# A hybrid attention and recurrence layer on one core: pools at multiples of 2048 bytes, and a queue plan with other durations

## The chip, the cores and the metric

The kernel runs on one core of a Trainium2 chip. The metric is the device time of one execution in microseconds (us). The engines are TensorE (PE; its weight loads are shown as PEld), VectorE (DVE), ScalarE (ACT), GpSimd (POOL) and SyncE (SP), which here only issues loads and stores.

## What is computed

One layer over 512 latent tokens and 256 context tokens, model width 2048, in float32. Cut to what matters:

```
hn = rmsnorm(h) * (1 + scale) + shift          # scale, shift, gate: silu(c) @ w_ada + b_ada
q, k, v, g, a_f, a_b, r, gr, m8, m9 = split(hn @ w_in)   # 14368 columns, latent and context
o = gla_bidir(q, k, v, log_sigmoid(a @ w_gla_a) / 16)    # 4 heads, dk 256, dv 512, both directions
y = rglru_bidir(conv4(r))                      # 2048 channels, 16 blocks, scans in both directions
y_gla = (rmsnorm(o) * silu(g)) @ w_o_gla
y_lru = (y * silu(gr)) @ w_o_rnn
out = rmsnorm(x + gate * ((sigmoid(m8) * y_gla + sigmoid(m9) * y_lru) @ w_out))
```

The context tokens pass through the same weights, and their last scan states start the latent scans.

## The kernel before

Every large product is made from float32r halves: a value is split into hi and lo, and `mm3` (L129) adds three matmuls, hi x hi, hi x lo, lo x hi. Weights come in pieces of 128 x 1024 (512 KB). `run` (L210) walks over a list of pieces: it loads some ahead (on SyncE's queue, into two raw buffers), splits each two pieces before its matmuls (`hilo`, L119: ScalarE writes whi, VectorE writes wlo, into a ring of three), and runs the piece's matmuls. There are 304 such splits. 24 matmuls of 512 columns make a piece of the output product.

Besides these pieces there is side work: generators in `self.side` (`rnn_block`, `gla_all`, `gate_row`), from which `run_side` (L163) takes the next step at every `yield` of a piece's matmuls. Whether it takes one is decided by a plan of times `self.T` and `self.rdy`, in which each helper (`act`, `tt`, `ts`, `stt`, `scan`, `mm`) adds its duration: it stops where VectorE or ScalarE is more than `lim` ahead of TensorE, or where a result that the next step waits for is not ready by `slack`. These numbers change only the order in which instructions are put in the queues. `flush_side` (L199) takes all that is left.

The stages, in order:
- `start` (L460), with a plan of its own (`at`, `pe`, `hot`, `todo`, `idle`): 8 tiles of x and 4 of the context are loaded and squared, `sums` (L569) adds over the partitions with fp32 matmuls against ones, `rstd` and `spread` make the reciprocal root mean square for every token; 64 pieces of the ada weights give scale and shift (`ada`, `mod`); `modulate` writes xhi, xlo, chi and clo; the key product (`key`) fills in between. Eight slots of 512 KB hold ada pieces: four of araw, four of tok.
- The recurrence's stage: `g_feat` for r and gr (xhi or chi moving, weights stationary) and `g_tok` for the values (weights moving, xhi, xlo, chi or clo stationary, 256 columns), with `rnn_block` as side work.
- The attention's stage: query, gates and the merge gates as pieces, `gla_all` as side work, head after head. `swap` (L408), called when the first piece of y is reloaded, flushes what is left of it.
- `g_out` for both branches, then `g_final` (L1487): four blocks j of 512 output columns, 8 pieces each. At j = 0 `loads` (L1501) fetches x in pieces 0 to 3 and three broadcast rows (gt, the gate; gb, its bias; gf, the last norm's gain) in pieces 4 to 6; GpSimd adds gb to gt in piece 6. `evac` (L1518) does for each of four token tiles: y = product * gt, x + y, the squares' sum on ScalarE, and for j < 3 the product with gf. Block 3 is finished tile by tile (`finish`, L1571).

SBUF pools lie one behind the other: const, raw, ring, xp (xhi, xlo; later o and the output stage's tiles), sm (small tiles, 1088 bytes a partition), cx (chi, clo), then start, or rnn, or st and gla, or st and yp. raw, ring and xp begin at multiples of 2048 bytes; chi, rnn, st and gla begin 1088 bytes past one, and yp at one again, by an unused tile `fill` of 960 bytes (L413).

Of the kernel before, what the change touches and what calls it, by code (L numbers as in the profile page):

```python
# [54 lines left out]
class Kern:  # L55
# [27 lines left out]
    def act(self, out, in_, func=AF.Copy, **kw):  # L83
        t = self.TABLE.get(func, self.table)
        sw = 1.3 if t != self.table else 0.0
        self.table = t
        self._op("act", self._n(in_) / 1200.0 + 0.2 + sw, out, in_)
        if "accum_out" in kw:
            self.rdy[kw["accum_out"].name] = self.T["act"] + 0.1
        return self.nc.scalar.activation(out=out, in_=in_, func=func, **kw)  # L90

    def tt(self, out, in0, in1, op):
        self._op("dve", self._n(out) / 960.0 + 0.08, out, in0, in1)
        return self.nc.vector.tensor_tensor(out=out, in0=in0, in1=in1, op=op)  # L94

    def ts(self, out, in0, s1, s2=None, op0=ALU.mult, op1=None):
        self._op("dve", self._n(out) / 960.0 + 0.08, out, in0, s1)
        if op1 is None:
            return self.nc.vector.tensor_scalar(out=out, in0=in0, scalar1=s1, scalar2=None, op0=op0)
        return self.nc.vector.tensor_scalar(out=out, in0=in0, scalar1=s1, scalar2=s2, op0=op0, op1=op1)  # L100

    def stt(self, out, in0, s, in1, op0, op1):
        self._op("dve", self._n(out) / 960.0 + 0.08, out, in0, in1)
        return self.nc.vector.scalar_tensor_tensor(out=out, in0=in0, scalar=s, in1=in1, op0=op0, op1=op1)  # L104

    def scan(self, out, a, u, init):
        self._op("dve", self._n(out) / 480.0 + 0.08, out, a, u)
# [15 lines left out]
    def mm(self, out, lhsT, rhs, start, stop, share=1):  # L123

        n = self._n(rhs)
        self._op("pe", (n / 2400.0 + 0.003 if n >= 256 else 0.213) / share, out, lhsT, rhs)
        self.nc.tensor.matmul(out, lhsT=lhsT, rhs=rhs, start=start, stop=stop, skip_group_check=True)  # L127
# [175 lines left out]
    def build(self):  # L303
# [31 lines left out]
        self.cp = const.tile([P, 32], F32, name="cp")  # L335
        self.sm = open_pool("sm", bufs=2)

# [16 lines left out]
        def to_rnn():  # L354
# [6 lines left out]
            nc.gpsimd.memset(self.mask.rearrange("p (b t) -> p b t", t=P)[:, :, 0:1], 0.0)  # L361
            self.rp = open_pool("rnn", bufs=1)
            self.side.append(self.decay_consts())
            self.gacc = self.rp.tile([P, 1024], F32, tag="gacc", name="gacc")

# [42 lines left out]
        def swap():  # L408
            self.flush_side()
            close_pool("gla")  # L410
            self.yp = yp = open_pool("yp", bufs=1)

            yp.tile([P, 240], F32, name="fill")  # L413
            R["y"] = [yp.tile([P, KT, 512], F32R, tag=t, name=t) for t in ("yhi", "ylo")]
# [45 lines left out]
    def start(self, sp, raw0, raw, prime):  # L460
# [74 lines left out]
        sb_free = [0.0]  # L535
        pr0 = self.ps.tile([P, 4, 2], F32, tag="sb", name="pr")

# [4 lines left out]
        def squares(i, t):  # L542
            if i < 8:
                q = self.ring.tile([P, 1024], F32R, tag="whi", name="sq").bitcast(F32)
                h = self.ring.tile([P, 1024], F32R, tag="wlo", name="sh").bitcast(F32)[:, 0:512]
                nc.scalar.activation(out=q, in_=tok[i], func=AF.Square)
                e = at("act", 1.06, t)
                nc.vector.tensor_tensor(out=h, in0=q[:, 0:512], in1=q[:, 512:1024], op=ALU.add)
                f = at("dve", 0.7, e)
                hot.append((lambda: f, lambda: sums(i, h, f)))  # L550
                return
# [17 lines left out]
        def sums(i, h, r):  # L569

            for j in range(4):
                nc.tensor.matmul(pr0[:, j, :], lhsT=h[:, j * P:(j + 1) * P], rhs=ones[:, 0:2],
                                 start=i == 0 and j == 0, stop=i == 7, skip_group_check=True)
            t = pe("pr", 0.9, r)
            if i == 7:
# [8 lines left out]
        def rstd(s, pr, t):  # L584
            n = width[s] // P
            q = sp.tile([P, 4], F32, tag="rq", name="rq")[:, 0:n]
            self.rstd(q, pr[:, :, 0], D, sp.tile([P, 2, 4], F32, tag="rt", name="rt")[:, :, 0:n])
            t = sb_free[0] = at("dve", 0.4, t + 0.1)
            at("act", 0.2, t)
# [5 lines left out]
            t = at("dve", 0.22 * n, t)  # L595
            hot.append((lambda: max(t, sb_free[0]), lambda: spread(s, g, t)))

        def spread(s, g, r):

            w = width[s]  # L600
            pr = self.ps.tile([P, w], F32, tag="sb", name="pr")
            nc.tensor.matmul(pr, lhsT=ones, rhs=g[:, 0:w], start=True, stop=True)
            t = pe("pr", w / 600 + 0.05, r, sb_free[0])
            nc.scalar.activation(out=rms[s], in_=pr, func=AF.Copy)
            sb_free[0] = tok_ok[s] = at("act", w / 1200 + 0.18, t + 0.1)

# [305 lines left out]
    def evac_v(self, j):  # L912
        def f(c, x0, x1):
            h, o = j // 2, (j % 2) * 256
            for i, t in enumerate((c, x0, x1)):
                s = self.rp.tile([P, 2, 256], F32, tag="stg", name="vt", bufs=2)
                self.act(s, t)
# [137 lines left out]
    def gate_row(self, acc, hf):  # L1055
        nc = self.nc
        for j in range(2):
            row = self.rp.tile([1, 512], F32, tag="grow", name="grow")
            yield self.dep(acc)
# [427 lines left out]
    def g_final(self, j):  # L1487
# [30 lines left out]
        def evac(t, then=None):  # L1518
# [5 lines left out]
            if then:  # L1524
                then()
            self.act(self.junk, xr, AF.Square, accum_out=self.fss[:, t, j:j + 1])
            if j < 3:
                self.tt(xr, xr, self.gf[:, c0:c0 + 512], ALU.mult)

        held = []  # L1530
        for pi in range(8):
            def mm(hi, lo, pi=pi):
# [8 lines left out]
                if j == 0:  # L1541
                    loads(pi)
                if j == 0 and pi == 6:
                    nc.gpsimd.tensor_tensor(out=self.gt, in0=self.gt, in1=self.gb, op=ALU.add)
                if j == 3 and pi >= 5:
                    held.append((pi, hi, lo))
                    if pi == 7:
                        rest = None
                        for t in range(4):
# [5 lines left out]
                for t in range(4):  # L1555
                    mm_k(t, pi, hi, lo)

            def post():
                if j < 3:
                    for t in range(4):  # L1560
                        evac(t)
                if j == 2:

                    f = self.fss
                    self.fsum = self.sm.tile([P, 4], F32, tag="fsum", name="fsum")
                    self.tt(self.fsum, f[:, :, 0], f[:, :, 1], ALU.add)
                    self.stt(self.fsum, self.fsum, EPS * D, f[:, :, 2], ALU.add, ALU.add)
            ps.append(Piece(a["w"][W_OUT + 8 * j + pi], mm, post if pi == 7 else None))
# [106 lines left out]
```

## Time and profile before

| | us |
|---|---|
| timed, median of 3 (lowest to highest) | 2302.43 (2301.64 to 2302.9) |
| the profiled execution | 2307.69 |
| its span, first to last instruction | 2306.0 |
| TensorE busy in the span | 2275.4 (99%) |
| VectorE, ScalarE, GpSimd busy | 1163.2, 1016.3, 105.5 |

Busy time of TensorE is counted from modelled ends of pipelined matmuls, so 99% does not say how dense they are; that is read from the times between starts. The chain that ended last and the waits tell which engine a stretch hangs on; a wait is put down to what came last.

### The profile page before, as it was taken

The page shows a single profiled execution, that of the slowest core. Times are in us where ns is not written, and L with a number is a line of the kernel's source. Part 1 is how long each engine was busy: PE and PEld are TensorE (multiplying, and loading weights), DVE is VectorE, ACT ScalarE, POOL GpSimd, SP SyncE. Part 2 cuts the span into 40 slices and gives each one's busy share as a digit, 9 for nine tenths or more (in the row PEclk, how much of TensorE's full clock was granted, in tenths as well). Part 3 has the DMA queues.
Part 4 walks back from the last instruction along what each step waited for, and adds up shares of the span by engine and source line. Part 5 has one row for each costly group of instructions (what it writes and reads, how often), then busy time and mean ns, then how long its engine had stood idle before and what let it go on. Part 6 is the DMA issues. An engine that isn't in the chain of part 4 may idle for free. (4 is left out here: it accounts for less than half of the span.)

```text
span 2306.0 us, 29334 instructions
## 1 busy us (share of the span) xinstructions
PE 2275.4 (99%) x12064; PEld 1928.6 (84%) x12064; DVE 1163.2 (50%) x1494; ACT 1016.3 (44%) x1334; POOL 105.5 (5%) x201
## 2 busy tenths in 40 slices
PE   8999999999999999999999999999999999999998
PEld 5588889989898988998888888888888888888786
DVE  3563245655566555646637637647623432443335
ACT  4343255454454455456556555555533312222223
POOL 0010000000000000000000000000000000000000
PEclk9999999999999999999999999999999999999999
DMA  9943222333333332233233233323335533334423
GB/s 392 375 165 127 92 79 90 129 120 110 105 106 128 124 112 81 100 113 115 90 106 124 83 106 127 119 74 110 132 114 197 192 123 115 127 113 150 173 101 119
DMA packets 85814, 303.02 MB, mean 131 GB/s; under 512 B 10416, under 2 KB 11568, under 8 KB 84784
## 3 DMA queue, kind: packets, MB, share of 16 engines
q1 hardware_dynamic: 72656, 255.78, 32.0%
q0 software_dynamic: 13024, 45.37, 5.5%
q8 instruction: 94, 1.54, 0.3%
q14 instruction: 40, 0.33, 0.0%
HBM read 270.69 MB, written 30.42 MB: 131 GB/s over the span
## 5 line engine op out<-in xcount | busy, mean ns | idle before, releaser
L94 DVE TENSOR_TENSOR wlo<-raw,whi 128x1024 fp32r<-128x1024 f32 x304 | 371.9, 1224 | 568.1 <-ACT whi L90 566.8
L90 ACT ACTIVATE whi<-raw 128x1024 fp32r<-128x1024 f32 x304 | 321.0, 1057 | 529.8 <-PE px L127 327.3
L127 PE MATMUL px<-xhi,whi 128*128 128x512 f32 x1408 | 551.5, 392 | 0.0
L127 PE MATMUL px<-xhi,wlo 128*128 128x512 f32 x1408 | 549.1, 390 | 0.0
L127 PE MATMUL px<-xlo,whi 128*128 128x512 f32 x1408 | 548.1, 389 | 0.0
L127 PEld LDWEIGHTS px<-xhi,wlo 128*128 128x128 f32 x1408 | 264.2, 188 | 57.5 <-DVE wlo L94 0.2
L127 PEld LDWEIGHTS px<-xhi,whi 128*128 128x128 f32 x1408 | 264.4, 188 | 53.9 <-issue 2.6
L127 PEld LDWEIGHTS px<-xlo,whi 128*128 128x128 f32 x1408 | 264.5, 188 | 51.6
L127 PE MATMUL px<-whi,xhi 128*128 128x256 f32 x512 | 144.8, 283 | 0.0
L127 PE MATMUL px<-wlo,xhi 128*128 128x256 f32 x512 | 144.8, 283 | 0.0
L127 PE MATMUL px<-whi,xlo 128*128 128x256 f32 x512 | 144.7, 283 | 0.0
L90 ACT ACT_TABLE_LOAD x100 | 128.3, 1283 | 1.7
L127 PE MATMUL px<-whi,mhi 128*128 128x512 f32 x256 | 100.7, 393 | 2.3 <-ACT whi L90 2.3
L127 PE MATMUL px<-wlo,mhi 128*128 128x512 f32 x256 | 101.0, 394 | 0.8 <-DVE wlo L94 0.8
L127 PE MATMUL px<-whi,mlo 128*128 128x512 f32 x256 | 100.7, 393 | 0.0
L127 PE MATMUL px<-yhi,whi 128*128 128x512 f32 x256 | 99.6, 389 | 0.0
L127 PE MATMUL px<-ylo,whi 128*128 128x512 f32 x256 | 99.6, 389 | 0.0
L127 PE MATMUL px<-yhi,wlo 128*128 128x512 f32 x256 | 99.6, 389 | 0.0
L127 PE MATMUL px<-ohi,whi 128*128 128x512 f32 x256 | 99.6, 389 | 0.0
L127 PE MATMUL px<-olo,whi 128*128 128x512 f32 x256 | 99.6, 389 | 0.0
L127 PE MATMUL px<-ohi,wlo 128*128 128x512 f32 x256 | 99.6, 389 | 0.0
L127 PEld LDWEIGHTS px<-wlo,xhi 128*128 128x128 f32 x512 | 98.1, 192 | 0.2
(327 smaller groups left out, 3963.6 us busy)
## 6 DMA issues: line engine op xcount, KB each, us to landing
raw<-in_w SPq DMA_DIRECT2D x304, 512.0 KB, 3.6
araw<-in_wss SPq DMA_DIRECT2D x35, 512.0 KB, 8.9
raw<-in_wgt SPq DMA_DIRECT2D x32, 512.0 KB, 4.2
tok<-in_wss SPq DMA_DIRECT2D x29, 512.0 KB, 8.9
kraw<-in_w POOLq DMA_DIRECT2D x16, 512.0 KB, 3.9
gS<-mst POOLq DMA_DIRECT2D x32, 256.0 KB, 2.5
gst<-gS POOLq DMA_DIRECT2D x32, 256.0 KB, 3.0
vS<-vt POOLq DMA_DIRECT2D x24, 256.0 KB, 2.6
```

The source lines that it names most:

```text
L90: return self.nc.scalar.activation(out=out, in_=in_, func=func, **kw)
L94: return self.nc.vector.tensor_tensor(out=out, in0=in0, in1=in1, op=op)
L127: self.nc.tensor.matmul(out, lhsT=lhsT, rhs=rhs, start=start, stop=stop, skip_group_check=True)
```

## The change

It does five things.
- **Pools.** sm is opened on the right side of SBUF, so that cx and all that follows begin at multiples of 2048 bytes; `fill` goes; the rnn pool's tags are laid out in a fixed order, those of 512, 1024 and 768 columns each together.
- **Durations of the plan.** VectorE's fixed part rises from 0.08 to 0.16 (0.21 with a scalar operand), ScalarE's by 0.07 for each operand scale or bias, a matmul's from 0.003 to 0.0135.
- **Start.** Two tiles of x are added before the matmuls against ones: four groups of eight records instead of eight groups. Their result and the spread's for x use PSUM banks px instead of sb. The start's own durations are set anew (1.87 instead of 0.9 for a group).
- **Output stage's loads.** gt and gb are loaded in pieces 0 and 1, gf in piece 4, and GpSimd's add comes in piece 3.
- **Output stage's evacuation.** Blocks 0 to 2 make only y and x + y at their end; the squares and the product with gf become side work `squares()`, taken at `yield`s between the next block's matmuls.

```diff
@@ act, tt, ts, stt, scan, mm @@
-        self._op("act", self._n(in_) / 1200.0 + 0.2 + sw, out, in_)
+        ap = sum(not isinstance(kw.get(k, 0.0), (int, float)) for k in ("scale", "bias"))
+        self._op("act", self._n(in_) / 1200.0 + 0.2 + 0.07 * ap + sw, out, in_)
...
-        self._op("dve", self._n(out) / 960.0 + 0.08, out, in0, in1)
+        self._op("dve", self._n(out) / 960.0 + 0.16, out, in0, in1)
...
-        self._op("pe", (n / 2400.0 + 0.003 if n >= 256 else 0.213) / share, out, lhsT, rhs)
+        self._op("pe", (n / 2400.0 + 0.0135 if n >= 256 else 0.213) / share, out, lhsT, rhs)
@@ build @@
-        self.sm = open_pool("sm", bufs=2)
+        self.sm = open_pool("sm", bufs=2, side="right")
...
+            self.gacc = rp.tile([P, 1024], F32, tag="gacc", name="gacc")
+            for n, w, d, m in (("wh", 512, F32R, 1), ("wl", 512, F32R, 1), ("wr", 512, F32, 1), ("gr", TX, F32, 3),
+                               ("sgr", TX, F32, 2), ("stg", 512, F32, 2), ("grow", 512, F32, 1), ("xr", TA, F32, 3),
+                               ("xh", TA, F32R, 1), ("xc", TA, F32, 1), ("xl", TA, F32R, 1)):
+                rp.tile([P, w], d, tag=n, name=n + "0", bufs=m)
...
-            yp.tile([P, 240], F32, name="fill")
@@ start @@
-        pr0 = self.ps.tile([P, 4, 2], F32, tag="sb", name="pr")
+        pr0 = self.px.tile([P, 4, 2], F32, tag="px", name="pr")
...
-                h = self.ring.tile([P, 1024], F32R, tag="wlo", name="sh").bitcast(F32)[:, 0:512]
                 nc.scalar.activation(out=q, in_=tok[i], func=AF.Square)
                 e = at("act", 1.06, t)
-                nc.vector.tensor_tensor(out=h, in0=q[:, 0:512], in1=q[:, 512:1024], op=ALU.add)
-                f = at("dve", 0.7, e)
-                hot.append((lambda: f, lambda: sums(i, h, f)))
+                if i % 2 == 0:
+                    half.append(self.ring.tile([P, 1024], F32R, tag="wlo", name="sh").bitcast(F32)[:, 0:512])
+                    nc.vector.tensor_tensor(out=half[0], in0=q[:, 0:512], in1=q[:, 512:1024], op=ALU.add)
+                    at("dve", 0.7, e)
+                else:
+                    h = half.pop()
+                    for u in (q[:, 0:512], q[:, 512:1024]):
+                        nc.vector.tensor_tensor(out=h, in0=h, in1=u, op=ALU.add)
+                        f = at("dve", 0.7, e)
+                    hot.append((lambda: f, lambda: sums(i, h, f)))
...
-            t = pe("pr", 0.9, r)
+            t = pe("pr", 1.87, r)
...
-            pr = self.ps.tile([P, w], F32, tag="sb", name="pr")
+            pool, tag = (self.ps, "sb") if s else (self.px, "px")
+            pr = pool.tile([P, w], F32, tag=tag, name="pr")
@@ g_final @@
+            if pi == 0:
+                nc.sync.dma_start(out=self.gt, in_=self.rS.partition_broadcast(P))
+            elif pi == 1:
+                nc.sync.dma_start(out=self.gb, in_=a["bgt"].partition_broadcast(P))
             elif pi == 4:
-                nc.sync.dma_start(out=self.gt, in_=self.rS.partition_broadcast(P))
-            elif pi == 5:
-                nc.sync.dma_start(out=self.gb, in_=a["bgt"].partition_broadcast(P))
-            elif pi == 6:
                 nc.sync.dma_start(out=self.gf, in_=a["gfin"].partition_broadcast(P))
...
-            self.act(self.junk, xr, AF.Square, accum_out=self.fss[:, t, j:j + 1])
-            if j < 3:
+            if j == 3:
+                self.act(self.junk, xr, AF.Square, accum_out=self.fss[:, t, j:j + 1])
+
+        def squares():
+            c0 = j * 512
+            for t in range(4):
+                xr = self.xres[:, t, c0:c0 + 512]
+                self.act(self.junk, xr, AF.Square, accum_out=self.fss[:, t, j:j + 1])
                 self.tt(xr, xr, self.gf[:, c0:c0 + 512], ALU.mult)
+                yield 0
...
-                if j == 0 and pi == 6:
+                if j == 0 and pi == 3:
                     nc.gpsimd.tensor_tensor(out=self.gt, in0=self.gt, in1=self.gb, op=ALU.add)
...
                 for t in range(4):
                     mm_k(t, pi, hi, lo)
+                    yield
...
                     for t in range(4):
                         evac(t)
+                    self.side.append(squares())
```

`ts` changes as `tt` does, `stt` goes to 0.21, `scan` to 0.16.

## Rows read from the trace of the kernel before

**Rows 1.** Stretches of the span: length, each engine's busy time (count), clock, DMA share, GB/s

```profile
115.00:173.00 58.00, 58.00 (x365) 48.80 (x362) 36.43 (x76) 27.85 (x54) 6.53 (x13) 1.00 0.49 167
...
1200.00:1400.00 200.00, 199.34 (x930) 166.29 (x929) 113.44 (x150) 116.08 (x146) 8.15 (x20) 1.00 0.29 100
...
2000.00:2200.00 200.00, 196.97 (x856) 162.32 (x855) 75.57 (x84) 47.80 (x56) 10.39 (x10) 0.98 0.41 143
```

**Rows 2.** What TensorE waited for, 231 to 1800 us: total, times, longest

```profile
PE pd L127 <- ACT Z L90: 2.0, 3, 0.7
PE rx L127 <- ACT grow L90: 1.5, 1, 1.5
PE pr L1061 <- ACT grow L90: 0.7, 1, 0.7
```

**Rows 3.** Timeline of the start: start, length, engine, line, operation, count

```profile
7.09 12.18 PE L572 MATMUL pr<-ones,sh 128*128 128x2 f32 x56 [7.09 <-DVE sh L548]
...
15.03 1.06 ACT L546 ACTIVATE sq<-tok 128x1024 f32<-128x1024 f32 x1 [0.19 <-DMA tok<-in_xT]
16.12 0.69 DVE L548 TENSOR_TENSOR sh<-sq 128x512 f32<-128x512 f32 x1 [0.56 <-ACT sq L546]
...
20.21 1.87 PE L572 MATMUL pr<-ones,sh 128*128 128x2 f32 x8
...
30.86 0.48 PE L832 MATMUL kx<-xhi,khi 128*128 128x512 f32 x1
```

**Rows 4.** Stretches of 5 us, 55 to 75 us, columns as in group 1

```profile
55.00:60.00 5.00, 5.00 (x32) 2.79 (x32) 1.83 (x8) 1.52 (x3) 0.00 (x0) 1.00 0.76 294
60.00:65.00 5.00, 5.00 (x30) 2.83 (x23) 3.00 (x5) 1.55 (x3) 0.54 (x1) 1.00 0.61 215
65.00:70.00 5.00, 5.00 (x26) 3.23 (x25) 1.03 (x2) 1.03 (x3) 0.54 (x1) 1.00 0.77 282
70.00:75.00 5.00, 2.89 (x14) 1.46 (x13) 3.12 (x10) 2.57 (x6) 0.54 (x1) 1.00 1.02 417
```

**Rows 5.** Timeline around the first output block's end

```profile
2145.89 0.42 SPq L1508 DMA_DIRECT2D gv<-in_bgt  x1
...
2155.27 5.55 POOL L1544 TENSOR_TENSOR gv<-gv 128x2048 f32<-128x2048 f32 x1 [59.49 <-DMA gv<-in_bgt]
...
2160.85 0.69 DVE L94 TENSOR_TENSOR yt<-px,gv 128x512 f32<-128x512 f32 x1 [4.49 <-POOL gv L1544]
...
2162.30 0.63 ACT L90 ACTIVATE gv<-xres 128x512 f32<-128x512 f32 x1 [7.20 <-DVE xres L94]
...
2165.16 0.63 ACT L90 ACTIVATE gv<-xres 128x512 f32<-128x512 f32 x1 [2.13 <-issue]
```

**Rows 6.** Two stretches of 10 us behind it, columns as in group 1

```profile
2169.94:2180.00 10.06, 7.03 (x18) 5.05 (x17) 5.10 (x6) 3.67 (x5) 0.00 (x0) 0.66 0.30 104
2180.00:2190.00 10.00, 10.00 (x46) 8.28 (x45) 2.45 (x2) 2.12 (x2) 0.00 (x0) 1.00 0.32 107
```

**Rows 7.** Timeline of TensorE, values' stage: first and last of two runs

```profile
914.15 0.28 PE L127 MATMUL pc<-whi,chi 128*128 128x256 f32 x1
...
916.15 0.28 PE L127 MATMUL pc<-whi,clo 128*128 128x256 f32 x1
916.27 0.28 PE L127 MATMUL px<-whi,xhi 128*128 128x256 f32 x1
...
921.91 0.28 PE L127 MATMUL px<-whi,xlo 128*128 128x256 f32 x1
```

**Rows 8.** Matmuls that read chi: count; ns min/median/max; first and last start

```profile
L127 PE MATMUL pc<-chi,whi x256: 276/280/283, 226.2 to 869.8; 128*128 128x256 f32 x128
```

**Rows 9.** Groups by line: count, busy us, mean ns, idle before

```profile
L94 DVE TENSOR_TENSOR wlo<-raw,whi 128x1024 fp32r<-128x1024 f32 x304 | 371.9, 1224 | 568.1 <-ACT whi L90 566.8 <-PE px L127 0.7
```

**Rows 10.** The attention's last products, and the first reload of y

```profile
L94 DVE TENSOR_TENSOR sgg<-pt,sgg x16: 659/683/692, 1220.6 to 1704.8; 128x512 f32<-128x512 f32 x16
...
1710.08 0.33 SPq L153 DMA_DIRECT2D raw<-yS  x1
```

More of the change, by code (lines that the diff above doesn't have):

```diff
@@ L92, in tt @@
     def tt(self, out, in0, in1, op):
-        self._op("dve", self._n(out) / 960.0 + 0.08, out, in0, in1)
+        self._op("dve", self._n(out) / 960.0 + 0.16, out, in0, in1)
         return self.nc.vector.tensor_tensor(out=out, in0=in0, in1=in1, op=op)
     def ts(self, out, in0, s1, s2=None, op0=ALU.mult, op1=None):
-        self._op("dve", self._n(out) / 960.0 + 0.08, out, in0, s1)
+        self._op("dve", self._n(out) / 960.0 + 0.16, out, in0, s1)
         if op1 is None:
@@ L102, in stt @@
     def stt(self, out, in0, s, in1, op0, op1):
-        self._op("dve", self._n(out) / 960.0 + 0.08, out, in0, in1)
+        self._op("dve", self._n(out) / 960.0 + 0.21, out, in0, in1)
         return self.nc.vector.scalar_tensor_tensor(out=out, in0=in0, scalar=s, in1=in1, op0=op0, op1=op1)
     def scan(self, out, a, u, init):
-        self._op("dve", self._n(out) / 480.0 + 0.08, out, a, u)
+        self._op("dve", self._n(out) / 480.0 + 0.16, out, a, u)
         return self.nc.vector.tensor_tensor_scan(
@@ L362, in to_rnn @@
             self.rp = open_pool("rnn", bufs=1)
+            rp = self.rp
+            self.gacc = rp.tile([P, 1024], F32, tag="gacc", name="gacc")
[3 more added lines that the diff above has]
+                rp.tile([P, w], d, tag=n, name=n + "0", bufs=m)
             self.side.append(self.decay_consts())
-            self.gacc = self.rp.tile([P, 1024], F32, tag="gacc", name="gacc")
         pcs[0].before = to_rnn
@@ L535, in start @@
         sb_free = [0.0]
-        pr0 = self.ps.tile([P, 4, 2], F32, tag="sb", name="pr")
+        pr0 = self.px.tile([P, 4, 2], F32, tag="px", name="pr")
+        half = []
         def load_tok(i, d):
@@ L572, in sums @@
                 nc.tensor.matmul(pr0[:, j, :], lhsT=h[:, j * P:(j + 1) * P], rhs=ones[:, 0:2],
-                                 start=i == 0 and j == 0, stop=i == 7, skip_group_check=True)
-            t = pe("pr", 0.9, r)
+                                 start=i == 1 and j == 0, stop=i == 7, skip_group_check=True)
+            t = pe("pr", 1.87, r)
             if i == 7:
@@ L587, in rstd @@
             self.rstd(q, pr[:, :, 0], D, sp.tile([P, 2, 4], F32, tag="rt", name="rt")[:, :, 0:n])
-            t = sb_free[0] = at("dve", 0.4, t + 0.1)
+            t = at("dve", 0.3, t + 0.1)
+            if s:
+                sb_free[0] = t
             at("act", 0.2, t)
@@ L595, in rstd @@
             t = at("dve", 0.22 * n, t)
-            hot.append((lambda: max(t, sb_free[0]), lambda: spread(s, g, t)))
+            hot.append((lambda: max(t, sb_free[0] if s else 0.0), lambda: spread(s, g, t)))
         def spread(s, g, r):
             w = width[s]
-            pr = self.ps.tile([P, w], F32, tag="sb", name="pr")
+            pool, tag = (self.ps, "sb") if s else (self.px, "px")
+            pr = pool.tile([P, w], F32, tag=tag, name="pr")
             nc.tensor.matmul(pr, lhsT=ones, rhs=g[:, 0:w], start=True, stop=True)
-            t = pe("pr", w / 600 + 0.05, r, sb_free[0])
+            t = pe("pr", w / 600 + 0.05, r)
             nc.scalar.activation(out=rms[s], in_=pr, func=AF.Copy)
-            sb_free[0] = tok_ok[s] = at("act", w / 1200 + 0.18, t + 0.1)
+            tok_ok[s] = at("act", w / 1200 + 0.18, t + 0.4)
+            if s:
+                sb_free[0] = tok_ok[s]
         blocks = START_BLOCKS
@@ L915, in f @@
             for i, t in enumerate((c, x0, x1)):
-                s = self.rp.tile([P, 2, 256], F32, tag="stg", name="vt", bufs=2)
+                s = self.rp.tile([P, 512], F32, tag="stg", name="vt", bufs=2).rearrange("p (a c) -> p a c", a=2)
                 self.act(s, t)
@@ L1057, in gate_row @@
         for j in range(2):
-            row = self.rp.tile([1, 512], F32, tag="grow", name="grow")
+            row = self.rp.tile([P, 512], F32, tag="grow", name="grow")[0:1]
             yield self.dep(acc)
@@ L1525, in evac @@
                 then()
-            self.act(self.junk, xr, AF.Square, accum_out=self.fss[:, t, j:j + 1])
-            if j < 3:
-                self.tt(xr, xr, self.gf[:, c0:c0 + 512], ALU.mult)
+            if j == 3:
[5 more added lines that the diff above has]
+                self.act(self.junk, xr, AF.Square, accum_out=self.fss[:, t, j:j + 1])
+                self.tt(xr, xr, self.gf[:, c0:c0 + 512], ALU.mult)
+                yield 0
+            if j == 2:
+                f = self.fss
+                self.fsum = self.sm.tile([P, 4], F32, tag="fsum", name="fsum")
+                self.tt(self.fsum, f[:, :, 0], f[:, :, 1], ALU.add)
+                self.stt(self.fsum, self.fsum, EPS * D, f[:, :, 2], ALU.add, ALU.add)
+                yield 0
         held = []
@@ L1547, in mm @@
                     if pi == 7:
+                        self.flush_side()
                         rest = None
@@ L1561, in post @@
                         evac(t)
[L1562 to L1567, printed above, removed]
+                    self.side.append(squares())
             ps.append(Piece(a["w"][W_OUT + 8 * j + pi], mm, post if pi == 7 else None))
```

## The prediction

> **What bounds the kernel now.** I read the page's busy shares first, then stretches of the span, then what TensorE waited for, and only then single instructions. The stretches [rows 1] show a kernel bound by TensorE: from 115 us on it is busy all the time or nearly (58.00 of 58 us, 199.34 of 200), at the full granted clock, while VectorE and ScalarE have slack. So an edit counts only through (a) the start, where TensorE has nothing to do, (b) waits that it meets later, (c) the time from one matmul to the next, (d) the end. In the middle the waits are small: 4.2 us in all between 231 and 1800 us [rows 2]. The one dent behind that lies between 2000 and 2200 us, where the mean granted clock is 0.98 [rows 1].
>
> **The base.** The profiled execution took 2307.69 us, of which 2306.0 are its span; the three timed runs have a median of 2302.43. The durations below are those of the profiled one; I add the differences to the median.
>
> **Start: fewer sums of squares.** Now each of 8 token tiles has its own four fp32 matmuls for the sums, two records each. 56 records take 12.18 us, 0.217 us a record, and TensorE runs them without a gap; the last group begins only at 20.21 and ends at 22.08 [rows 3]. The change adds two tiles on VectorE first and so makes four groups of eight records: 32 records x 0.217 = 6.9 us of TensorE leave. Not all of that can be gained, as TensorE would then wait for tiles. The last tile's square ends at 15.03 + 1.06 = 16.09; today one add of 0.69 follows, then there will be two (16.81, 17.5), and a group of 1.87 us ends at 19.4: 2.7 us before 22.08 [rows 3]. The reciprocal square root, the spread over partitions, the first modulated tile and the first key matmul (30.86 now) hang on this, so they move by about that. The spread's result goes to a px bank and no longer keeps the ada rows' transposes out of the one bank sb, which helps a little more.
> Will the stream of loads allow it? Its share is 1.02 where it is full, but it falls to 0.76, 0.61 and 0.77 in the three stretches from 55 to 70 us [rows 4]: slots were given back late, because TensorE was behind. That is (0.26 + 0.41 + 0.25) x 5 us = 4.6 us of room, so a shift of 3 us fits. The hand-kept times of the start (1.87 for a group of sums where 0.9 stood) make its plan agree with the chip, and may remove more of that dip. Bounds: 0 (the stream decides after all) and 6.9 us (all that was removed). I take **-3.0**, near the 2.7 that the rows give for the chain.
>
> **End: the first output block's evacuation.** The sum of gt and the bias bgt is made by GpSimd in 5.55 us, and it starts at 2155.27, as bgt's load was issued only at 2145.89, in piece 5. VectorE's first product of the block begins at 2160.85, just behind it. Then each of four tiles goes VectorE, VectorE, ScalarE (square), VectorE in order, so that ScalarE's squares stand 2.86 us apart (2162.30, 2165.16, and two more) [rows 5]; the next weight splits are queued behind them on both engines. TensorE runs dry at 2169.94: in the 10.06 us from there it runs 18 matmuls at a mean clock of 0.66, where the 10 us after hold 46 with the two at the edges [rows 6]. 18 at that rate are 4.0 us, so 6.0 us are lost, to the wait and to the fall from 2.4 to 1.2 GHz behind it.
> The change issues gt and bgt in pieces 0 and 1, and the GpSimd sum in piece 3, so it ends long before the block does. At the block's end only two VectorE operations a tile remain (8 x 0.69 = 5.5 us, by the first of them [rows 5]); squares and the gain's products become side work, spread over the next block's matmuls. A split is made two pieces of 24 matmuls ahead, that is 10 us, and 5.5 us fit into this. The price: gt and bgt now share SyncE's queue with two tiles of x, each 1 MB or 2.5 us at 417 GB/s [rows 4]. A weight load behind them lands up to 5 us later in two pieces; the two pieces of cover hide it. The GpSimd sum moves beside other weight splits; if VectorE had to wait for all of its 5.55 us, the same cover would still hold it. Blocks 1 and 2 did not stall before, so nothing more is gained there. The tail after the last block, its four tiles in turn, keeps its operations and their order. So **-6.0**; bounds 0 and -6.0.
>
> **The pools' places.** In the built kernel before, raw, ring and xp begin at multiples of 2048 bytes already, and yp does by its fill. What moves is what lay behind the 1088 bytes of sm: chi and clo, and the rnn, st and gla pools. For rnn and gla, moving and stationary operand move together. For chi and clo they do not: today whi (at a multiple) meets chi (64 bytes past a multiple of 128). The trace has both cases within one stage, with the same instruction, the same 256 columns: 18 matmuls of whi against chi or clo start from 914.15 to 916.15, 117.6 ns apart; the 48 that follow, of whi against xhi or xlo, both at multiples, from 916.27 to 921.91, 120.0 ns apart [rows 7]. If the equal places are the reason, then the move makes chi's matmuls 2.4 ns dearer. There are 1920 of them: 768 with chi or clo moving in the projections, 768 with them stationary, 384 in the keys; the first two are three kinds of 256 each, of which [rows 8] shows one, the keys three of 128. The bounds are 0 (another reason) and 1920 x 2.4 = 4.6 us. Only those of the values come in long runs beside others at 120; the rest stand in runs of 12 or 24 between matmuls of 512 columns, where the time apart is not settled yet. 768 x 2.4 = 1.8 for the first, half of (1152 x 2.4 = 2.8) for the rest: **+3.2**. No row shows a gain from the move.
> The Trainium skill speaks against this term: TensorE: Matmul & The Clock Gate, section Part 2: What happens when you issue a matmul, says that TensorE has two independent read ports, so loading the next weights takes nothing from the running matmul. By that the places of the two operands would not matter and this term would be 0. The trace does not bear that out so far, as the two runs differ and the addresses are what differs.
>
> **The planner's durations.** The queue order in the middle comes from a plan. Its figure for a 512-column matmul goes from 216.3 to 226.8 ns (+4.9%), for a 256-column one from 109.7 to 120.2 (+9.6%), for a 1024-element VectorE operation from 1.147 to 1.227 (+7.0%), which the trace has at 1.224 [rows 9]. So per matmul the side work is placed about where it was; ScalarE's steps, whose cost hardly changes, come a little earlier. What TensorE waits for in the middle (three waits for Z, one for the gate row) does not come from these figures: the first takes the PSUM banks that the instruction just before must still give back, the second waits behind a store. Of 4.2 us [rows 2] I expect **0**, with 2 us either way.
>
> Sum: -3.0 - 6.0 + 3.2 + 0 = -5.8, so 2302.43 - 5.8 = **2296.6 us**, 0.25% faster.
>
> **Rivals.**
> (1) Places make no difference. For it: one run of each kind is a thin base, and they differ in the pool that they read, too. Against it: within the stage nothing but the addresses differs [rows 7]. (The Trainium skill's rule on the read ports, above, would give this case.) Then 2296.6 - 3.2 = 2293.4.
> (2) The end's gain is lost. The early loads of gt and bgt hold up the weight loads by more than the 10 us of cover, and the stall only changes its place. Against it: 5 us is less than 10. Then 2296.6 + 6.0 = 2302.6.
> (3) Slower: the side work of the linear attention does not end before its pool is closed. Its last product (16 in all, the last from 1704.8, some 0.68 long) precedes the first reload of y, issued at 1710.08, by only 4.6 us [rows 10], and at that point whatever is left is forced into the queues. VectorE's planned steps grow by 7.0% against 4.9% for the matmuls they are counted in: 2.1%. One head takes about 161 us ((1704.8 - 1220.6)/3), four 645; if VectorE made up the whole chain, it would be 13.5 us late and overrun by 9. With such a wait the clock falls as at 2170 us, some 2.5 us more, so 2296.6 + 11.5 = 2308.1. It decides from an overrun of the 4.6 us. Against it: ScalarE has half of the chain, and its planned steps shrink against the matmuls.
>
> **How the numbers follow.** Forecast 0.50, rival (1) 0.30, (2) 0.08, (3) 0.12. Low end: all 6.9 us of the start, the end's 6.0, no pitch term: 2289.5. High end: rival (2), rounded up to 2303. This leaves out most of rival (3) and a little at the low end. A measurement of this kernel tells 0.2% (4.6 us) from no change: faster means below 2297.8. The forecast's own spread (start 0 to 6.9, pitch 0 to 4.6) puts about 0.65 of its case below, nearly all of rival (1): 0.50 x 0.65 + 0.30 x 0.95 = 0.61. Slower: most of rival (3), 0.10. Same: the rest, 0.29.
>
> **What would show it.** Right: 32 records of sums, first key matmul near 28 us; no TensorE wait and a clock of 1.00 from 2160 to 2200; runs of whi against chi at 120 ns. Wrong: a first key matmul at 30 us or later, or the dip in the loads still there and TensorE behind as before; a new wait of ScalarE's splits for loads near 2130 us; waits of TensorE near 1705 us; runs against chi still at 117.6 ns.

## The result and the profile after

The changed kernel takes 2323.11 us (median of 6 runs, 2320.86 to 2325.44); the kernel before, on the same chip, 2302.03. The ratio is 1.0088, with a 95% interval of 1.0077 to 1.0099: 21 us slower, where 2296.6 and "faster" were forecast. The profiled execution took 2323.0 us, its span 2321.3.

**Stretches.** Three stretches of the changed kernel, columns as in [rows 1]:

```profile
600.00:800.00 200.00, 196.28 (x1223) 176.59 (x1222) 115.25 (x127) 100.28 (x131) 7.63 (x12) 0.98 0.35 113
1600.00:1800.00 200.00, 192.12 (x868) 159.54 (x869) 98.94 (x115) 92.93 (x118) 11.81 (x24) 0.97 0.39 131
2000.00:2200.00 200.00, 200.00 (x885) 165.68 (x884) 83.49 (x91) 50.15 (x59) 10.52 (x12) 1.00 0.44 148
```

The dent of [rows 1] between 2000 and 2200 us is gone (885 matmuls against 856, clock 1.00). There are two new ones: 600 to 800, and above all 1600 to 1800, where TensorE is idle for 7.9 us (200 - 192.12) and its mean granted clock is 0.97.

**Waits.** What TensorE waited for, 231 to 1800 us, the view of [rows 2]: total, times, longest.

```profile
PE pt L1451 <- DVE on L100: 6.7, 3, 4.1
PE rx L128 <- ACT grow L91: 3.0, 1, 3.0
PE px L128 <- ACT whi L91: 2.6, 1, 2.6
PE pd L128 <- ACT Z L91: 2.0, 3, 0.7
PE pr L1080 <- ACT grow L91: 1.5, 2, 0.8
PE po L128 <- DVE ht L95: 0.8, 1, 0.8
PE px L128 <- DVE wlo L95: 0.5, 1, 0.5
```

17.1 us where [rows 2] have 4.2. Those for Z are unchanged; those for the gate's row (grow) have grown from 2.2 to 4.5 us; those for on (a head's output after its norm), ht (an operand of the attention), whi and wlo (the halves of the weights) are new.

**Where the time went.** I compared the two traces at equal work: each matmul has a place in the total, if all before it are counted at 0.2267 us for 512 columns and 0.120 for 256, and others in proportion. The table shows when each kernel comes to such a place.

| work done, us | before | after | after is behind by |
|---|---|---|---|
| 60 | 79.9 | 77.4 | -2.6 |
| 120 | 134.3 | 133.0 | -1.3 |
| 600 | 615.0 | 615.3 | +0.2 |
| 625 | 643.2 | 647.6 | +4.4 |
| 1000 | 1019.2 | 1025.2 | +6.0 |
| 1550 | 1576.4 | 1581.0 | +4.5 |
| 1575 | 1601.4 | 1614.0 | +12.6 |
| 1650 | 1676.7 | 1689.2 | +12.5 |
| 1725 | 1752.4 | 1774.1 | +21.7 |
| 2100 | 2127.3 | 2149.0 | +21.7 |
| 2175 | 2208.7 | 2224.0 | +15.3 |

So: a lead at the start, part of it soon given back; a slow loss up to 1000 us; three sudden losses, 4.2 us near 620, 8.0 near 1600 and 9.2 between 1700 and 1735; and 6.4 us won at 2170. The sum, 15.3, is the difference of the two spans. It is less than 21 because the profiled execution of before was itself 5.3 us slower than its median. That turns out to matter below.

**The loss near 1600 us.** ScalarE's timeline in the changed kernel (start, length, engine, line, operation, and in brackets the idle time before it with what ended it), then TensorE's:

```profile
1598.30 1.28 ACT L91 ACT_TABLE_LOAD   x1 [10.31 <-DMA oS<-sgg]
1599.59 1.08 ACT L91 ACTIVATE sgg<-px 128x512 f32<-128x512 f32 x2
1600.56 2.00 ACT L91 ACTIVATE whi<-raw 128x1024 fp32r<-128x1024 f32 x2
```

```profile
1601.67 0.50 PE L128 MATMUL px<-xhi,whi 128*128 128x512 f32 x1 [2.64 <-ACT whi L91]
...
1602.93 0.50 PE L128 MATMUL px<-xhi,wlo 128*128 128x512 f32 x1 [0.53 <-DVE wlo L95]
...
1603.97 0.61 PE L128 MATMUL px<-xhi,whi 128*128 128x512 f32 x1
```

ScalarE stands still for 10.31 us. It wants to write a new tile sgg, the output gate of a head, and its place is still being stored (oS<-sgg) from the head before, which had only just been finished. Two weight splits are queued behind it, and TensorE runs out of weights. Then the clock falls as well: the matmuls from 1603.97 on take 0.61 us instead of 0.39.

**The loss after 1700 us.** VectorE's and TensorE's rows there:

```profile
1720.54 0.17 DVE L101 TENSOR_SCALAR otmp<-oss 128x4 f32<-128x4 f32 x1 [14.58 <-ACT dg L91]
...
1723.07 1.41 DVE L100 TENSOR_SCALAR on<-po,ors 128x512 f32<-128x512 f32 x2
```

```profile
1719.34 0.39 PE L128 MATMUL po<-ht,Al 128*128 128x512 f32 x1
1723.87 1.97 PE L1451 MATMUL pt<-ident,on 128*128 128x128 f32 x8 [4.15 <-DVE on L100]
1726.43 2.37 PE L1451 MATMUL pt<-ident,on 128*128 128x128 f32 x8 [0.59 <-DVE on L100]
1728.45 0.77 PE L128 MATMUL px<-xhi,whi 128*128 128x512 f32 x1
```

The last head's products po run here without one projection matmul between them, up to 1719.34; then come its norm on VectorE and its transposes, each waiting for the one before. The projections go on at 1728.45. This is the flush: what is left of the attention is forced into the queues in one lump before its pool is closed. In [rows 10] the last sgg<-pt started at 1704.8, 5.3 us before the first reload of y; now:

```profile
L95 DVE TENSOR_TENSOR sgg<-pt,sgg x16: 665/686/692, 1227.4 to 1728.8; 128x512 f32<-128x512 f32 x16
L154 SPq DMA_DIRECT2D raw<-yS x8: 319/320/320, 1704.9 to 1778.6; - x8
```

From its first product to its last the attention takes 501.4 us instead of 484.2, and the last one starts 23.9 us after the first reload was issued.

### The profile page after: what moved, and what is told of

It reads as the page before. It is cut to its first block, busy times and chain, and to the rows that moved or that the text cites. A ratio compares the mean times of both kernels' runs of the same rounds, so it can differ in the third digit from the quotient of the medians.

```text
span 2321.3 us, 29284 instructions
## 1 busy us (share of the span) xinstructions
PE 2276.1 (98%) x12032; PEld 1929.9 (83%) x12032; DVE 1166.7 (50%) x1498; ACT 1020.5 (44%) x1337; POOL 104.6 (5%) x201
## 4 chain that ended last, share of the span: by engine, by line
PE 83%; issue 11%; DMA 3%; DVE 2%; ACT 2%; POOL 0%; SPq 0%; DVEq 0%; ACTq 0%; POOLq 0%
PE px L128 63%; PE pc L128 5%; PE kx L851 4%; PE po L128 3%; PE kc L851 2%; PE rx L128 1%; PE pd L128 1%; DMA tok<-in_wss 1%; PE pcs L128 1%; PE pa L692 1%; PE rc L128 1%; DMA araw<-in_wss 0%; DMA kraw<-in_w 0%; DVE Z L109 0%; PE pt L1451 0%
```

## Experiments

Two theories to begin with. A: the planner's durations do it; the plan now places the attention's steps later against the matmuls, until the code has to force them. B: the pools' places, or the changed order of the start, shift the queues. Each kernel is compared with the kernel before, run beside it on the same chip:

| run | what it is | us | ratio to before, 95% interval |
|---|---|---|---|
| e1_no_durations | the change without the durations | 2300.57 | 0.9992 (0.9983 to 1.0001) |
| e2_durations_alone | before, with the durations | 2318.03 | 1.0070 (1.0057 to 1.0082) |
| e3_places_alone | before, with the places | 2304.55 | 1.0010 (1.0001 to 1.0019) |
| e4_end_alone | before, with the new end | 2300.98 | 0.9992 (0.9984 to 1.0001) |
| e5_start_alone | before, with the new start | 2299.10 | 0.9985 (0.9976 to 0.9994) |
| e6_no_vector_durations | the change, VectorE's figures as before | 2311.53 | 1.0043 (1.0029 to 1.0056) |
| e7_chi_off | e1, chi and clo moved by 64 bytes | 2296.68 | 0.9975 (0.9965 to 0.9985) |
| e8_x_off | e1, x and all behind it moved by 64 bytes | 2301.93 | 0.9998 (0.9989 to 1.0007) |
| e9_slack_1 | the change, attention's margin 1.0 | 2306.91 | 1.0021 (1.0012 to 1.0030) |
| e10_vector_durations_alone | before, with VectorE's figures | 2346.62 | 1.0193 (1.0179 to 1.0207) |
| e11_ring_off | e1, some weight tiles moved by 64 bytes | 2311.91 | 1.0045 (1.0032 to 1.0059) |
| e12_slack_1_grow_2 | e9, the gate's row in two buffers | 2303.07 | 1.0002 (0.9993 to 1.0011) |

### The four parts apart

**e1_no_durations**: the change with the planner's lines as before.

```diff
-        self._op("dve", self._n(out) / 960.0 + 0.16, out, in0, in1)
+        self._op("dve", self._n(out) / 960.0 + 0.08, out, in0, in1)
...
-        self._op("pe", (n / 2400.0 + 0.0135 if n >= 256 else 0.213) / share, out, lhsT, rhs)
+        self._op("pe", (n / 2400.0 + 0.003 if n >= 256 else 0.213) / share, out, lhsT, rhs)
```

> The whole change but the planner's durations (all six figures as before). Theory A (the durations place the linear attention's side work too late, so that it is forced into the queues in three places, where TensorE then waits): the three losses of the changed kernel at 620, 1600 and 1705 to 1730 us (4.2, 8.0 and 9.2 us more lag than before) are gone, so 2323.1 - 21.4 = 2301.7 us, or 2295.3 if the 6.4 us of the end that the one profile of before had are lost in every execution. Rival B (the places of the pools, or the start's other order, shift the queues): 2315 us or more.

**e2_durations_alone**: the kernel before, with just those lines changed (the diff above, the other way round).

> The kernel before with nothing but the six durations changed. Theory A: the three losses are all here, 2302.0 + 21.4 = 2323.4 us (2318 to 2327), with TensorE's waits near 1600 and 1720 us. Rival B (places or start): within 3 us of before, 2299 to 2305.

2300.6 and 2318.0: theory A holds, B falls. In the trace of e2 the waits of the changed kernel are back, to the tenth for the largest:

```profile
PE pt L1433 <- DVE on L100: 6.7, 3, 4.1
PE rx L128 <- ACT grow L91: 2.1, 1, 2.1
...
PE px L128 <- ACT whi L91: 2.0, 2, 1.0
```

Alone the durations cost 16 us (13 to 19); put back into the whole change, 2323.1 - 2300.6 = 22.5 (22 by the ratios, 1.0088 against 0.9992). Most of this difference lies in two places, where the same waits are a little longer in the changed kernel and the clock follows only there. The stretches around 620 and 1600 us, the changed kernel first, then e2:

```profile
617.00:632.00 15.00, 11.28 (x37) 7.48 (x36) 3.35 (x3) 4.30 (x6) 1.02 (x2) 0.77 0.23 71
1590.00:1612.00 22.00, 18.83 (x75) 14.76 (x75) 11.39 (x21) 8.47 (x10) 1.25 (x5) 0.92 0.35 120
```

```profile
617.00:632.00 15.00, 12.22 (x52) 8.41 (x51) 4.26 (x4) 6.18 (x10) 1.03 (x2) 1.00 0.31 100
1590.00:1612.00 22.00, 20.45 (x90) 16.29 (x89) 12.79 (x20) 11.16 (x13) 0.80 (x1) 1.00 0.39 129
```

A wait of 3.0 us for the gate's row pulls the mean granted clock of its stretch down to 0.77; one of 2.1 us leaves it at 1.00. At equal work each place costs the changed kernel 3.2 us more than e2: 6.4 of the difference. Why the waits are longer is not shown. At 620 it is the store of the gate's row: ScalarE idles 3.47 us before its second copy, in e2 2.53. That wait also differs between executions of the same queue order: 2.2 us in the profile of before, 0.9 in that of e4, whose edit comes only behind it.

**e3_places_alone**: the kernel before, with sm on the right, the rnn pool's tiles laid out first, and no fill.

```diff
-        self.sm = open_pool("sm", bufs=2)
+        self.sm = open_pool("sm", bufs=2, side="right")
...
-            yp.tile([P, 240], F32, name="fill")
```

> The kernel before with nothing but the pools' places changed. The order in the queues stays. My prediction's step: matmuls of 256 columns that read whi and chi go from 117.5 to 120.0 ns apart, 1920 x 2.4 = 4.6 us at most. The changed kernel's trace also has the first matmuls after a switch of width cheaper, about 2.5 us in all; if the places do that too, the sum is +2, 2304 us. If the places cost what I wrote, +3 to +4.6: 2305 to 2306.6. Rival (places make no difference): 2302.

2304.55, by the ratio 2.3 us slower (0.2 to 4.4).

**e4_end_alone**: the kernel before, with the new g_final.

```diff
-            elif pi == 4:
+            if pi == 0:
...
-                if j == 0 and pi == 6:
+                if j == 0 and pi == 3:
...
+                    self.side.append(squares())
```

> The kernel before with nothing but the last projection's evacuation changed (early loads of gt and bgt, squares as side work). My prediction's step: -6.0, 2296 us. Rival: the profiled execution of before took 2307.7 us against a median of 2302, and its 6 us at 2170 us may be what the median does not have; then 0 to -1, 2301 to 2302 us.

2300.98, by the ratio 1.8 us faster (3.7 faster to 0.2 slower): nearer to the rival. The traces say why. e3 has the end of before, untouched and with the same order in the queues, yet no such hole as in [rows 6]. First the stretch, then the GpSimd sum, both in e3:

```profile
2170.00:2180.00 10.00, 9.24 (x41) 7.33 (x40) 4.28 (x4) 4.54 (x6) 0.00 (x0) 1.00 0.34 109
```

```profile
2154.30 4.61 POOL L1549 TENSOR_TENSOR gv<-gv 128x2048 f32<-128x2048 f32 x1 [56.96 <-DMA gv<-in_bgt]
```

41 matmuls instead of 18, and the clock at 1.00. At equal work the hole is 6.4 us in the profile of before, 1.1 in that of e3 and 0.4 in that of e5, which has the same end too: its size differs from execution to execution, and the median has little of it. What makes it large is not settled. The sum, 5.55 us in [rows 5] and 4.61 here, may be part of it, but e2 with 4.61 us lost 3.9.

**e5_start_alone**: the kernel before, with four groups of sums and the spread in a px bank.

```diff
-                nc.vector.tensor_tensor(out=h, in0=q[:, 0:512], in1=q[:, 512:1024], op=ALU.add)
-                f = at("dve", 0.7, e)
-                hot.append((lambda: f, lambda: sums(i, h, f)))
+                if i % 2 == 0:
...
+                    for u in (q[:, 0:512], q[:, 512:1024]):
+                        nc.vector.tensor_tensor(out=h, in0=h, in1=u, op=ALU.add)
```

> The kernel before with nothing but the start changed (four groups of sums instead of eight, the spread's result in a px bank). My prediction's step: -3.0, 2299.6 us. Rival (the stream of loads decides the first 115 us; in the kernel with all but the durations the lead is 1.1 us at 40 us of span and nothing near 57 us): 0 to -1, 2301.6 to 2302.6, with a lead of 2 to 3 us at the first key matmul that is given back before 115 us.

2299.1, 3.5 us faster (1.4 to 5.5). The rival, to which I leaned by then, falls; the lead is kept. Start, places and end together make -3.5 + 2.3 - 1.8 = -3.0; e1, which has all three, measures -1.8 (3.9 faster to 0.2 slower).

### Why the durations hurt

**e9_slack_1**: the whole change, with one number altered.

```diff
-            self.lim, self.slack = 3.0, 1.5
+            self.lim, self.slack = 3.0, 1.0
```

> The whole change, with one number altered: in the attention's stage the margin by which the plan holds a step back behind its inputs is 1.0 us instead of 1.5 (line 398 of the changed kernel). Theory A (true, longer durations plus that margin at every step add up along the chain until it does not fit into its stage): the losses near 1600 and 1705 to 1730 us go, 8.0 + 9.2, the one at 620 stays: 2323.1 - 17.2 = 2306 us (2303 to 2309). Rival (the new durations spoil the order as such, whatever the margin): 2315 us or more.

2306.9, as theory A had it. The waits for on, ht, whi and wlo are gone; the attention ends in time again, and the one loss left is that at 620:

```profile
L95 DVE TENSOR_TENSOR sgg<-pt,sgg x16: 662/691/692, 1222.5 to 1707.9; 128x512 f32<-128x512 f32 x16
L154 SPq DMA_DIRECT2D raw<-yS x8: 326/327/327, 1715.5 to 1762.4; - x8
```

```profile
617.00:632.00 15.00, 11.34 (x35) 7.50 (x34) 2.99 (x3) 4.15 (x6) 1.02 (x2) 0.77 0.24 75
1590.00:1612.00 22.00, 22.00 (x105) 18.64 (x104) 15.23 (x15) 10.60 (x13) 0.00 (x0) 1.00 0.30 96
1700.00:1735.00 35.00, 35.00 (x164) 28.98 (x163) 14.59 (x16) 12.13 (x13) 3.23 (x6) 1.00 0.53 180
```

**e12_slack_1_grow_2**: as e9, with a second buffer for the gate's row (it gets its place in the fixed layout too).

```diff
-            row = self.rp.tile([P, 512], F32, tag="grow", name="grow")[0:1]
+            row = self.rp.tile([P, 512], F32, tag="grow", name="grow", bufs=2)[0:1]
```

> As the run with the margin of 1.0, and the gate's row in two buffers instead of one, so that the second row need not wait for the first one's store; the order of all queues is the same. If the loss of 4.2 us at 620 is that store: 3 to 4.2 us less than that run, 2302 to 2303 us. Rival (TensorE waits there for something else): the same as that run.

2303.07, 3.8 us less than e9: it was the store. In the changed kernel the two row sums stand next to each other, with no projection matmul between, and the second copy to grow must wait until the first has been stored:

```profile
620.37 1.02 PE L1080 MATMUL pr<-gacc,ones 128*1 128x512 f32 x2
622.06 1.02 PE L1080 MATMUL pr<-gacc,ones 128*1 128x512 f32 x2 [0.68 <-ACT grow L91]
626.12 0.79 PE L128 MATMUL rx<-xh,wh 128*128 128x512 f32 x1 [3.04 <-ACT grow L91]
```

The planner counts neither these two matmuls nor the store, so it does not choose where they fall against the projections, and any change of its figures can move them. The row on ScalarE that decides, in the changed kernel and then in e12:

```profile
625.49 0.59 ACT L91 ACTIVATE grow<-pr 1x512 f32<-1x512 f32 x1 [3.47 <-DMA rS<-grow]
```

```profile
623.52 0.59 ACT L91 ACTIVATE grow<-pr 1x512 f32<-1x512 f32 x1 [1.11 <-PE pr L1080]
```

Even so, e12, with the durations, the smaller margin and the second buffer, is no faster than the kernel before (1.0002), and not told apart from e1, which has the old durations (0.9992).

**e10_vector_durations_alone**: the kernel before, with VectorE's four lines alone (from tt to scan) changed.

> The kernel before with only VectorE's four figures changed, TensorE's and ScalarE's as before. Theory A (the chain's planned length against the matmuls' planned length decides): the chain is planned longer, the matmuls are not, so it must be later than with all six changed, and the loss larger than that run's 15.4 us: 2320 to 2340 us. Rival (it is TensorE's figure that does the harm): 2302 to 2310 us.

2346.6, 44 us slower, beyond the upper end of what A expected, on A's side. With TensorE's figure unchanged the chain is planned longer and the matmuls are not. At equal work the trace loses 30 us between 1450 and 1700 us of work, in the attention, but also 11 us between 950 and 1000, behind one wait of 6.4 us for a split (wh) in the recurrence, which A had not named.

**e6_no_vector_durations**: the reverse, all of the change but those four lines.

> The whole change, but VectorE's four figures of the planner as before; ScalarE's and TensorE's stay new. Theory A2 (what delays the attention's side work is VectorE's added 0.08 to 0.13 us an operation, counted up along the chain; TensorE's longer figure alone gives the side work more room): no forced step, 2299 to 2302 us. Rival A3 (any of the six does it, as the plan was tuned as a whole): 2310 us or more.

2311.5: outside A2's 2299 to 2302, and by the number the rival's. The trace says where. The attention's losses are indeed gone (from 1000 us of work to the end it falls behind the counted work by 7.7 us, e1 by 6.8). But against e1 a new loss of some 11 us has come up in the recurrence, between 400 and 1000 us of work:

```profile
PE rx L128 <- ACT wh L91: 4.0, 4, 1.8
PE pr L1080 <- ACT grow L91: 2.7, 2, 2.0
```

TensorE comes to the recurrence's matmuls before their weights are split. So A2 holds for the attention and fails for the kernel. The reading that fits, argued and not shown step by step: the steps are now placed too early, as the plan believes in a VectorE that is at least 0.08 us an operation faster than it is, while its matmuls have the true length. Before, both figures were too small, and the errors offset each other; with both raised (e9) the recurrence has no such waits but the gate's row, and the attention needs the smaller margin.

### The places

**e7_chi_off**: e1, with 64 bytes in front of chi.

```diff
         cpool = open_pool("cx", bufs=1)
+        cpool.tile([P, 16], F32, name="pad")
```

> All but the durations, and chi and clo moved 64 bytes up, so that they no longer stand where whi and wlo stand (modulo 128 bytes). My prediction's theory of places: matmuls of 256 columns of whi against chi go back from 120.0 to 117.5 ns, 1920 x 2.4 = 4.6 us at most, about 2 of them given back at the switches of width: 2300.6 - 2.5 = 2298 us (2296 to 2299.5). Rival (the 2.4 ns come from something else that moved with them): 2300.6 and 120.0 ns.

2296.7, within the 2296 to 2299.5 of the theory, and the fastest kernel of this study, 0.25% below before (0.15% to 0.35%); against its own before it lies 4 us below e1. First and last of 24 matmuls of whi and wlo against chi and clo, in the changed kernel, then in e7:

```profile
918.67 0.28 PE L128 MATMUL pc<-whi,chi 128*128 128x256 f32 x1
...
921.43 0.28 PE L128 MATMUL pc<-whi,clo 128*128 128x256 f32 x1
```

```profile
917.83 0.28 PE L127 MATMUL pc<-whi,chi 128*128 128x256 f32 x1
...
920.54 0.28 PE L127 MATMUL pc<-whi,clo 128*128 128x256 f32 x1
```

2.76 us over 23 steps are 120.0 ns, as forecast for the changed kernel; 2.71 are 117.8, near the 117.6 of [rows 7].

**e8_x_off**: e1, with the same 64 bytes in front of xhi, so that chi stands where it stands in e7, and x is moved as well.

```diff
+        xp.tile([P, 16], F32, name="pad")
         self.xhi = xp.tile([P, KT, TX], F32R, tag="xhi", name="xhi")
```

> All but the durations, and the input's and all later pools moved 64 bytes up against the weights' ring. By the theory of places now the 1536 matmuls of 256 columns against xhi and xlo are also 2.4 ns cheaper (3.7 us), beside those against chi: 2300.6 - 2.5 - 3.7 = 2294.4 us (2293 to 2297), unless the switches of width give it back. The 512-column matmuls stay at 226.7 ns. Rival (places make no difference): 2300.6.

2301.9: outside of both. The 256-column matmuls got cheaper still, but the 512-column ones did not stay as they were. The same 24 matmuls, and 15 of 512 columns in the output projection:

```profile
911.38 0.28 PE L127 MATMUL pc<-whi,chi 128*128 128x256 f32 x1
...
913.98 0.28 PE L127 MATMUL pc<-whi,clo 128*128 128x256 f32 x1
...
2049.72 0.39 PE L127 MATMUL px<-ohi,whi 128*128 128x512 f32 x1
...
2052.93 0.39 PE L127 MATMUL px<-ohi,wlo 128*128 128x512 f32 x1
```

2.60 over 23 steps are 113.0 ns; 3.21 over 14 are 229.3, against 226.7. The many more matmuls of 512 columns give everything back. And the 24 matmuls read whi and chi at the very addresses of e7, where they took 117.8: the places of a matmul's own two operands do not settle its pitch, the time from one start to the next.

**e11_ring_off**: e1 with x and chi at multiples of 128 bytes, and the weight tile moved by 64 bytes in it for the pieces with 256-column matmuls only.

```diff
+        t = self.ring.tile([P, 1040], F32R, tag=tag, name=name)
+        at = (64 * (-i % 3) + (64 if tag == "wlo" else 0)) % 128
+        o = 0 if at == off else 16
+        return t[:, o:o + 1024]
```

> All but the durations; chi, clo, xhi and xlo stand at multiples of 128 bytes, and the weights' tiles begin 64 bytes past one for the pieces of the projections with 256-column matmuls (values, and recurrence with chi), at a multiple for all others. The kernel with x moved had 113.9 ns for the 2304 matmuls of the values and 115.4 against chi, but 228.9 for 512 columns, to the end. If the place of the weights against x and chi does it: 2300.6 - 2304 x 6.1 ns - 768 x 4.6 ns + 768 x 2 ns = 2284.6 us (2283 to 2289). Rival (it is the place of x itself): 2300.6 or above.

2311.9, slower by 10 us (7 to 14): a miss by 27. The weights stand 64 bytes from x where they should and together with x elsewhere, modulo 128, as planned. The 256-column matmuls of the values did get cheaper (116.5 ns on average, 120.0 in e1); but the matmuls of 512 columns, which now read tiles at other multiples of 128 than of 2048, are dearer: some 4,570 of them against xhi and xlo took 18.5 us in all beyond 226.7 ns each, 4.3 in e1, and those of the output projections, against o and y, 231.3 ns on average where e1 has 226.6. So "the same modulo 128" is not the rule. What the rule is stays open.

## Why the prediction was wrong, step by step

**The planner's durations (0, with 2 either way): the step that failed.** They cost 16 us alone and 22.5 in the change. I compared one VectorE operation, of 1024 elements, +7.0%, with the matmul's +4.9%, and took the difference, 2%, for the chain. "So per matmul the side work is placed about where it was" was wrong, and two rows show by how much. The first product sgg<-pt of the third head, before and then in the changed kernel:

```profile
1550.86 0.69 DVE L94 TENSOR_TENSOR sgg<-pt,sgg 128x512 f32<-128x512 f32 x1 [0.81 <-PE pt L1432]
```

```profile
1579.16 0.69 DVE L95 TENSOR_TENSOR sgg<-pt,sgg 128x512 f32<-128x512 f32 x1 [2.15 <-PE pt L1451]
```

From the first head's first product (1220.6 and 1227.4) that is 330.3 us before and 351.7 after: 6.5% longer, not 2.1%, and ahead of the first of the two losses. What I left out: a fixed 0.08 us weighs far more on the attention's own operations, 0.613 to 0.693 for 512 elements (+13%), 0.084 to 0.164 for the 4-element steps of the norm, which the trace has at 0.16 to 0.18; and at every step that waits for inputs there is the margin of 1.5 us. With a margin of 1.0 (e9) the same stretch takes 333.8 us, 1.1% more than before. How the 6.5% divide between the small operations and the rest is not shown. And I looked for waits that the old plan had, not for those that a later plan would make.

**Rival (3), 0.12, 2308.1 us: the right mechanism, mis-sized.** Its place, the flush before y's pool, and its deciding margin, 4.6 us, were right; the overrun was put at 9. Two things were missing. The flush is not the only point where work is forced: the code also waits for a head's end before it evacuates a later head's gate, and there ScalarE's queue stands for 10.31 us with the splits behind it. And the gate's row, in plain view in [rows 2], was set aside as "does not come from these figures", though its wait depends on what is queued between its two halves, and e12 shows what this cost: 3.8 us.

**The end (-6.0): right in the trace, wrong as a term.** TensorE no longer runs dry: 46 matmuls where [rows 6] have 18.

```profile
2169.94:2180.00 10.06, 10.06 (x46) 8.35 (x45) 4.36 (x6) 2.73 (x4) 0.00 (x0) 1.00 0.46 163
```

At equal work this gave 6.4 us. But the term was taken from an execution that was 5.3 us slower than the median, and added to the median. Alone the step is worth 1.8 us. I had written both numbers down and did not ask what the 5.3 consisted of: the other profiles with the end of before lose 0.4 to 3.9 us there.

**The start (-3.0): right.** Alone -3.5 (1.4 to 5.5). The records of the sums go from 64 to 32. The way there was a little off: the last group starts at 18.43 instead of 17.5 and ends at 20.30, the first key matmul comes at 28.72 ("near 28"):

```profile
18.43 1.87 PE L586 MATMUL pr<-ones,sh 128*128 128x2 f32 x8
...
28.72 0.50 PE L851 MATMUL kx<-xhi,khi 128*128 128x512 f32 x1
```

The dip in the loads is partly filled, 0.92, 0.65 and 1.03 where [rows 4] have 0.76, 0.61 and 0.77; but e2, with the start of before, has 0.86, 0.64 and 0.99, so this is not shown to be the start's doing.

**The places (+3.2): right in sign and kind.** Whi against chi takes 120.0 ns, as forecast; the price alone is 2.3 us (0.2 to 4.4). In the trace of e3 the loss up to 1000 us of work is 3.0 more than before's, and 1.2 come back afterwards. Some 0.8 of that is that the first ten 512-column matmuls behind the attention's other ones cost less (the third to the tenth 227 to 230 ns on average instead of 227 to 233); I had no row for that gain. Rival (1) falls with e3 and e7. The Trainium skill's rule (TensorE: Matmul & The Clock Gate, Part 2: What happens when you issue a matmul) that the two read ports are independent does not cover this: places alone moved the pitch between 113.0 and 120.0 ns. But my own reason, equal places modulo 128 bytes, fell too, with e8 and e11.

**Rival (2)** did not come up: e4 shows no new wait for weights.

**The range.** Its upper end, 2303, left out rival (3) as the sum stood; at 2308.1 that rival too lay far below the 2323.1 measured, as it counted one forced place of two and none of the gate's row.

## What to carry to other kernels

Truer figures in a planner are a new plan, not a small correction: look for the places where unfinished work is forced (a pool's closing, a slot's reuse), and add up each fixed amount over the chain's smallest operations and its margins before calling the change neutral. Figures that are wrong together can offset each other; correct them together, and then the margins that were set under them (here 1.5 to 1.0 us gave back 16 us, and still left the kernel no faster than before). And before a hole in one profiled execution becomes a gain, compare that execution's time with the median.

## What the runs showed of the hardware

- The start-to-start time of 256-column fp32r matmuls depended on where tiles stand in SBUF: in a run of 24 in the values' stage 120.0 ns with all at multiples of 2048 bytes, 117.8 with chi moved by 64 bytes (e7), 113.0 with x moved as well (e8); that of 512 columns, in the output projection, 226.6 on average in e1, and 229.3 in a run of 15 with x moved. The mechanism is open.
- The same GpSimd addition of 128x2048 took 5.55 us in the profiled execution of before and 4.60 or 4.61 in those of the changed kernel, e3 and e4.
- Waits of 3.0 us (for the gate's row) and of 2.6 and 0.5 us in a row (for a split) were followed by matmuls at the lower clock; one of 2.1 us in the same place as the first (e2) was not.
